# Embedding gather with position add: indices turned on VectorE instead of TensorE, GpSimd as leader, second position load issued earlier

## The chip, the cores and the metric

One core of one Trainium2 chip. The metric is device time in microseconds (us), the median of repeated executions. All executions told here are undisturbed (clock 1.00).

## The reference

```python
batch, seq_len, vocab_size, d_model = 32, 512, 50000, 512
token_embed = embedding_table[indices]          # float32 rows of 2 KB
return (token_embed + position_embed).astype(np.float32)
```

16,384 rows are gathered (33.6 MB), a position row is added to each, and 33.6 MB are stored. The position table is 1 MB, the indices 128 KB as 64-bit words.

## The kernel before

Position p*4+k of a sequence lies on partition p. A *slot* holds one sequence (128 partitions x 4 x 512 float32); there are 23 slots. GpSimd issues one indirect DMA of 128 rows (256 KB) per pair (sequence b, quarter k), 128 in all, with at most 10 in flight. VectorE adds the position row, ScalarE issues the stores.

```python
# ScalarE: loads
nc.scalar.dma_start(out=idx0[:, 0, :], in_=idx_first[:, 0, :]).then_inc(s_first, 16)
load_pos(0)                                    # 512 KB: quarters 0 and 1
nc.scalar.dma_start(out=idx0[:, 1:, :], in_=idx_first[:, 1:, :]).then_inc(s_next, 16)
nc.scalar.dma_start(out=idx_raw[:], in_=...).then_inc(s_raw, 16)   # all indices, 128 KB
nc.scalar.wait_ge(s_pos[0], 16)
load_pos(1)                                    # 512 KB: quarters 2 and 3
# GpSimd
nc.gpsimd.affine_select(out=ident[:], ...)     # identity, for the matmuls
nc.gpsimd.wait_ge(s_first, 16)
for g, (b, k) in enumerate(order):
    if g == half: nc.gpsimd.wait_ge(s_next, 16)
    if g == FIRST * K: nc.gpsimd.wait_ge(s_prep, 2 + K + J)        # indices turned
    ...
    ins = nc.gpsimd.indirect_dma_start(out=slots[b % SLOTS][:, k, :], in_=table, ...)
    ins = ins.then_inc(s_gather[g % LANES], 16)                    # LANES = 10
    if g >= LANES: ins._wait_ge(s_gather[g % LANES], rounds(g - LANES))
# TensorE: four transposes of the indices as float32
# VectorE
for g, (b, k) in enumerate(order):
    if g == 7: tensor_copy(idx_f <- idx_raw)                       # int32 to float32
    if g == 9: four tensor_copy(idx_t <- turned)                   # PSUM float32 to int32
    if b == 0: tensor_copy(pos_ps[:, k, :] <- pos_sb[:, k, :])     # positions into PSUM
    slot += pos_ps[:, k, :]                                        # waits for gather g
# ScalarE: one store for each half sequence (512 KB) as its adds are done
# (cut: the last sequence, and the first halves of sequences 0 and 1, go in quarters)
```

The first four sequences take their indices straight from a small load (idx0). The other 28 need them turned: they are loaded with contiguous rows, and must come to lie with one position per partition.

Of the kernel before, what the change touches and what calls it, by code (L numbers as in the profile page):

```python
# [7 lines left out]
P = 128  # L8
K = 4
# [3 lines left out]
Q = 32  # L13


@with_exitstack
def kernel(
    ctx: ExitStack,
    tc: tile.TileContext,
    indices: bass.AP,  # L20
    embedding_table: bass.AP,
    position_embed: bass.AP,
    out: bass.AP,
):






    nc = tc.nc
    f32 = mybir.dt.float32
    i32 = mybir.dt.int32
    add = mybir.AluOpType.add

    B, S = indices.shape
    V, D = embedding_table.shape
    assert S == P * K and B == 32
    assert V < (1 << 24), "an index passes through float32"
    J = P // Q  # L40


    idx_words = indices.bitcast(i32)
    idx_first = idx_words[0:FIRST].rearrange("b (p w) -> p b w", p=P)
    idx_rows = idx_words.rearrange("b (j w) -> (b j) w", j=J)
    out_rows = out.rearrange("b (p k) d -> b p k d", k=K)
    pos_rows = position_embed.rearrange("(p k) d -> p k d", k=K)
    table = embedding_table[:, :]

    def sbuf(name, shape, dtype):  # L50
        return ctx.enter_context(tc.tile_pool(name="p_" + name, bufs=1)).tile(
            shape, dtype, name=name
        )

    def psum(name, shape, dtype):
        pool = tc.tile_pool(name="p_" + name, bufs=1, space=bass.MemoryType.PSUM)
        return ctx.enter_context(pool).tile(shape, dtype, name=name)

    idx0 = sbuf("idx0", [P, FIRST, 2 * K], i32)
    idx_raw = sbuf("idx_raw", [P, Q * K, 2], i32)  # L60
    ident = sbuf("ident", [P, P], f32)
    idx_f = sbuf("idx_f", [P, Q, K], f32)
    idx_t = sbuf("idx_t", [P, K, B], i32)
    pos_sb = sbuf("pos_sb", [P, K, D], f32)
    slots = [sbuf(f"slot{n}", [P, K, D], f32) for n in range(SLOTS)]
    turned = psum("turned", [Q, K, B, J], f32)
    pos_ps = psum("pos_ps", [P, K, D], f32)



    half = K // 2
    order = [(b, k) for h in range(2) for b in range(FIRST)
             for k in range(h * half, (h + 1) * half)]
    order += [(b, k) for b in range(FIRST, B) for k in range(K)]
    stores = []
    for g, (b, k) in enumerate(order):
        if (b <= 1 and k < half) or b == B - 1:
            stores.append((g + 1, b, k, 1))
        elif k % half == half - 1:
            stores.append((g + 1, b, k + 1 - half, half))  # L80

    sem = tc.alloc_semaphore
    s_first, s_next, s_raw = sem("s_first"), sem("s_next"), sem("s_raw")
    s_pos = [sem(f"s_pos{h}") for h in range(2)]
    s_gather = [sem(f"s_gather{n}") for n in range(LANES)]

    reused = range(B - SLOTS)
    s_out, s_rest = sem("s_out"), sem("s_rest")

    s_prep, s_ps, s_add = sem("s_prep"), sem("s_ps"), sem("s_add")  # L90

    def rounds(g):
        return 16 * (g // LANES + 1)

    def load_pos(h):
        part = slice(h * half, (h + 1) * half)
        nc.scalar.dma_start(out=pos_sb[:, part, :], in_=pos_rows[:, part, :]).then_inc(
            s_pos[h], 16
        )

    with tc.tile_critical(sync_engine=nc.vector.engine, no_gpsimd_drain=True):  # L101


        nc.scalar.dma_start(out=idx0[:, 0, :], in_=idx_first[:, 0, :]).then_inc(
            s_first, 16
        )
        load_pos(0)
        nc.scalar.dma_start(out=idx0[:, 1:, :], in_=idx_first[:, 1:, :]).then_inc(
            s_next, 16
        )  # L110
        nc.scalar.dma_start(
            out=idx_raw[:], in_=idx_rows.rearrange("r (s w) -> r s w", w=2)
        ).then_inc(s_raw, 16)
        nc.scalar.wait_ge(s_pos[0], 16)
        load_pos(1)


        nc.gpsimd.affine_select(  # L118
            out=ident[:], in_=nc.const_aps.tensor(1.0, [P, P], f32),
            pattern=[[-1, P]], compare_op=mybir.AluOpType.is_equal, fill=0.0,  # L120
            base=0, channel_multiplier=1,
        ).then_inc(s_prep, 1)
        nc.gpsimd.wait_ge(s_first, 16)
        for g, (b, k) in enumerate(order):
            if g == half:
                nc.gpsimd.wait_ge(s_next, 16)
            if g == FIRST * K:
                nc.gpsimd.wait_ge(s_prep, 2 + K + J)
            if b == SLOTS and k == 0:
                done = sum(1 for x in stores if x[1] in reused)  # L130
                nc.gpsimd.wait_ge(s_out, 16 * done)
            if b < FIRST:
                where = idx0[:, b, 2 * k : 2 * k + 1]
            else:
                where = idx_t[:, k, b : b + 1]
            ins = nc.gpsimd.indirect_dma_start(  # L136
                out=slots[b % SLOTS][:, k, :],
                out_offset=None,
                in_=table,
                in_offset=bass.IndirectOffsetOnAxis(ap=where, axis=0),  # L140
            ).then_inc(s_gather[g % LANES], 16)
            if g >= LANES:
                ins._wait_ge(s_gather[g % LANES], rounds(g - LANES))
        nc.gpsimd.drain()


        nc.tensor.wait_ge(s_prep, 2)
        for k in range(K):
            nc.tensor.transpose(  # L149
                turned[:, k].rearrange("p b j -> p (b j)"), idx_f[:, :, k], ident[:]  # L150
            ).then_inc(s_prep, 1)


        for g, (b, k) in enumerate(order):
            if g == 7:
                nc.vector.tensor_copy(  # L156
                    out=idx_f[:].rearrange("r p k -> r (p k)"), in_=idx_raw[:, :, 0]
                )._wait_ge(s_raw, 16).then_inc(s_prep, 1)
            if g == 9:
                nc.vector.wait_ge(s_prep, 2 + K)  # L160
                for j in range(J):
                    nc.vector.tensor_copy(  # L162
                        out=idx_t[j * Q : (j + 1) * Q, :, :], in_=turned[:, :, :, j]
                    ).then_inc(s_prep, 1)
            if b == 0:
                nc.vector.tensor_copy(out=pos_ps[:, k, :], in_=pos_sb[:, k, :])._wait_ge(  # L166
                    s_pos[k // half], 16
                ).then_inc(s_ps, 1)
                nc.vector.wait_ge(s_ps, k + 1)
            part = slots[b % SLOTS][:, k, :]  # L170
            nc.vector.tensor_tensor(  # L171
                out=part, in0=part, in1=pos_ps[:, k, :], op=add
            )._wait_ge(s_gather[g % LANES], rounds(g)).then_inc(s_add, 1)


        rest = 0
        for adds, b, at, n in stores:
            done = s_out if b in reused else s_rest
            rest += b not in reused
            nc.scalar.dma_start(  # L180
                out=out_rows[b][:, at : at + n, :],
                in_=slots[b % SLOTS][:, at : at + n, :],
            )._wait_ge(s_add, adds).then_inc(done, 16)
    tc.no_sync_barrier()
    nc.scalar.wait_ge(s_rest, nc.scalar.to_reg(16 * rest))
# [30 lines left out]
```

## Time and profile before

| | value |
|---|---|
| time, median of 6 | 182.02 us (181.74 to 182.42) |
| profiled span | 178.1 us |
| GpSimd busy | 121.8 us (68%) |
| VectorE busy | 91.4 us (51%) |
| moved | 68.34 MB, mean 384 GB/s over the span |

The row of the page that says most is the rate in 40 slices of 4.45 us each:

```profile
GB/s 122 234 329 359 375 378 364 385 410 413 416 416 419 419 419 420 419 420 419 419 420 420 419 419 418 419 418 419 420 419 420 418 420 420 420 419 421 417 258 0
```

The rate takes nine slices (40 us) to pass 400 and thirteen to reach 419, and then stays near there until the last two slices.

### The profile page before, as it was taken

The numbers are of one execution on the slowest core, as the hardware profiler recorded it, in microseconds if no ns is written. First come the engines' busy times: TensorE is split into PE (matmuls) and PEld (weight loads), VectorE is DVE, ScalarE is ACT, GpSimd is POOL, SyncE is SP. The second block draws the span as 40 slices with busy tenths as digits, with TensorE's granted clock in tenths as the row PEclk, the third lists the DMA queues.
The fourth block names the chain that finished last, engine by engine and source line by source line (L and its number), as shares of the span: only waits on it lengthen the run. The fifth ranks groups of instructions, "written<-read, shape, count | busy, mean of one in ns | idle before, by whom it ended". The sixth has DMA issues, their size and how long they took to land.

```text
span 178.1 us, 415 instructions
## 1 busy us (share of the span) xinstructions
PE 1.0 (1%) x4; PEld 0.4 (0%) x4; DVE 91.4 (51%) x137; POOL 121.8 (68%) x133
## 2 busy tenths in 40 slices
PE   0000100000000000000000000000000000000000
PEld 0000000000000000000000000000000000000000
DVE  0445973455556555555556455555556555554510
POOL 3777777777777777777777777777777777774000
DMA  4899999999999999999999999999999999999960
GB/s 122 234 329 359 375 378 364 385 410 413 416 416 419 419 419 420 419 420 419 419 420 420 419 419 418 419 418 419 420 419 420 418 420 420 420 419 421 417 258 0
DMA packets 21011, 68.34 MB, mean 384 GB/s; under 512 B 3728, under 2 KB 3856, under 8 KB 21008
## 3 DMA queue, kind: packets, MB, share of 16 engines
q10 hardware_dynamic: 10768, 34.76, 48.6%
q0 software_dynamic: 10240, 33.56, 48.1%
q14 instruction: 3, 0.02, 0.0%
HBM read 34.75 MB, written 33.55 MB: 384 GB/s over the span
## 4 chain that ended last, share of the span: by engine, by line
POOL 65%; issue 23%; DMA 5%; DVE 2%; ACTq 0%; DVEq 0%
POOL slot L136 65%; DMA slot<-in_embedding_table_dram,idx_t 4%; DVE slot L171 2%; DMA idx<-in_indices_dram 1%; ACTq L211 0%; DVEq L101 0%
## 5 line engine op out<-in xcount | busy, mean ns | idle before, releaser
L136 POOL DMA_INDIRECT slot<-in_embedding_table_dram,idx_t x112 | 106.0, 946 | 34.1 <-issue 34.1
L171 DVE TENSOR_TENSOR slot<-slot,pos_ps 128x512 f32<-128x512 f32 x128 | 87.7, 687 | 73.8 <-issue 57.8
L136 POOL DMA_INDIRECT slot<-in_embedding_table_dram,idx x16 | 15.3, 958 | 6.0 <-issue 4.6
L166 DVE COPY pos_ps<-pos_sb 128x512 f32<-128x512 f32 x4 | 2.7, 685 | 4.9 <-DMA pos_sb<-in_position_embed_dram 4.9
L162 DVE CAST idx_t<-turned 32x128 int32<-32x128 f32 x4 | 1.1, 280 | 0.1
L149 PE MATMUL turned<-ident,idx_f 128*32 128x128 f32 x4 | 1.0, 413 | 17.6 <-issue 17.6
L118 POOL TENSOR_SCALAR_AFFINE_SELECT ident<-const-float32-1.0 128x128 f32<-128x128 f32 x1 | 0.3, 282 | 0.7 <-DVEq L101 0.7
L149 PEld LDWEIGHTS turned<-ident,idx_f 128*32 128x32 f32 x4 | 0.4, 131 | 17.7 <-issue 17.6
L200 POOL MEMSET const-float32-0.0<- 128x1 f32 x1 | 0.1, 99 | 0.3 <-issue 0.3
L156 DVE CAST idx_f<-idx_raw 128x128 f32<-128x128 int32 x1 | 0.2, 220 | 0.0
L200 POOL MEMSET const-uint8-127<- 128x1 uint8 x1 | 0.1, 116 | 0.0
L200 POOL MEMSET const-bfloat16-1.0<- 128x1 bf16 x1 | 0.1, 110 | 0.0
L200 POOL MEMSET const-float32-1.0<- 128x1 f32 x1 | 0.1, 102 | 0.0
## 6 DMA issues: line engine op xcount, KB each, us to landing
out_dram<-slot ACTq DMA_DIRECT2D x60, 512.0 KB
out_dram<-slot ACTq DMA_DIRECT2D x8, 256.0 KB
slot<-in_embedding_table_dram,idx_t POOLq DMA_INDIRECT x112
pos_sb<-in_position_embed_dram ACTq DMA_DIRECT2D x2, 512.0 KB, 4.7
slot<-in_embedding_table_dram,idx POOLq DMA_INDIRECT x16
idx_raw<-in_indices_dram ACTq DMA_DIRECT2D x1, 128.0 KB
idx<-in_indices_dram ACTq DMA_DIRECT2D x1, 4.0 KB, 1.6
idx<-in_indices_dram ACTq DMA_DIRECT2D x1, 12.0 KB
```

Source lines behind the costliest of these rows:

```text
L118: nc.gpsimd.affine_select(out=ident[:], in_=nc.const_aps.tensor(1.0, [P, P], f32), pattern=[[-1, P]], compare_op=mybir.AluOpType.is_equal, ...
L136: ins = nc.gpsimd.indirect_dma_start(out=slots[b % SLOTS][:, k, :], out_offset=None, in_=table, in_offset=bass.IndirectOffsetOnAxis(ap=whe ...
L149: nc.tensor.transpose(turned[:, k].rearrange("p b j -> p (b j)"), idx_f[:, :, k], ident[:]).then_inc(s_prep, 1)
L156: nc.vector.tensor_copy(out=idx_f[:].rearrange("r p k -> r (p k)"), in_=idx_raw[:, :, 0])._wait_ge(s_raw, 16).then_inc(s_prep, 1)
L162: nc.vector.tensor_copy(out=idx_t[j * Q : (j + 1) * Q, :, :], in_=turned[:, :, :, j]).then_inc(s_prep, 1)
L166: nc.vector.tensor_copy(out=pos_ps[:, k, :], in_=pos_sb[:, k, :])._wait_ge(s_pos[k // half], 16).then_inc(s_ps, 1)
L171: nc.vector.tensor_tensor(out=part, in0=part, in1=pos_ps[:, k, :], op=add)._wait_ge(s_gather[g % LANES], rounds(g)).then_inc(s_add, 1)
L200: nc = _bacc.Bacc("TRN2", target_bir_lowering=False, num_devices=1)
```

## The change

Its intent: take the turning of the indices off three engines. If 32 partitions hold 32 sequences, VectorE's transpose of 32 x 32 blocks does the whole turning in one instruction, in int32; identity, cast to float32, four matmuls and four casts back go. The index load becomes four loads for that. GpSimd releases the other engines at the start in place of VectorE, and the second half of the position table is issued right behind the index loads instead of after the first half has landed.

```diff
-    with tc.tile_critical(sync_engine=nc.vector.engine, no_gpsimd_drain=True):
+    with tc.tile_critical(sync_engine=nc.gpsimd.engine, no_gpsimd_drain=True):
...
-        nc.scalar.dma_start(
-            out=idx_raw[:], in_=idx_rows.rearrange("r (s w) -> r s w", w=2)
-        ).then_inc(s_raw, 16)
-        nc.scalar.wait_ge(s_pos[0], 16)
+        for j in range(J):
+            nc.scalar.dma_start(
+                out=idx_raw[j * B : (j + 1) * B, :], in_=idx_rows[:, j, :]
+            ).then_inc(s_raw, 16)
         load_pos(1)
-        nc.gpsimd.affine_select(out=ident[:], ...)
...
-                nc.gpsimd.wait_ge(s_prep, 2 + K + J)
+                nc.gpsimd.wait_ge(s_idx, 1)
...
-        (four nc.tensor.transpose, one cast to float32, four casts back)
+                nc.vector.transpose(
+                    out=idx_t[:],
+                    in_=idx_raw[:].rearrange("r (q k w) -> r k q w", k=K, w=2)[:, :, :, 0],
+                )._wait_ge(s_raw, 16 * J).then_inc(s_idx, 1)
```

More of the change, by code (lines that the diff above doesn't have):

```diff
@@ L38 @@
     assert S == P * K and B == 32
-    assert V < (1 << 24), "an index passes through float32"
     J = P // Q
+    assert B == Q, "indices are turned in squares of 32"
     idx_words = indices.bitcast(i32)
     idx_first = idx_words[0:FIRST].rearrange("b (p w) -> p b w", p=P)
-    idx_rows = idx_words.rearrange("b (j w) -> (b j) w", j=J)
+    idx_rows = idx_words.rearrange("b (j w) -> b j w", j=J)
     out_rows = out.rearrange("b (p k) d -> b p k d", k=K)
@@ L59 @@
     idx0 = sbuf("idx0", [P, FIRST, 2 * K], i32)
-    idx_raw = sbuf("idx_raw", [P, Q * K, 2], i32)
-    ident = sbuf("ident", [P, P], f32)
-    idx_f = sbuf("idx_f", [P, Q, K], f32)
+    idx_raw = sbuf("idx_raw", [P, 2 * Q * K], i32)
     idx_t = sbuf("idx_t", [P, K, B], i32)
@@ L65 @@
     slots = [sbuf(f"slot{n}", [P, K, D], f32) for n in range(SLOTS)]
-    turned = psum("turned", [Q, K, B, J], f32)
     pos_ps = psum("pos_ps", [P, K, D], f32)
@@ L88 @@
     s_out, s_rest = sem("s_out"), sem("s_rest")
-    s_prep, s_ps, s_add = sem("s_prep"), sem("s_ps"), sem("s_add")
+    s_idx, s_ps, s_add = sem("s_idx"), sem("s_ps"), sem("s_add")
     def rounds(g):
@@ L110 @@
         )
-        nc.scalar.dma_start(
-            out=idx_raw[:], in_=idx_rows.rearrange("r (s w) -> r s w", w=2)
-        ).then_inc(s_raw, 16)
-        nc.scalar.wait_ge(s_pos[0], 16)
+        for j in range(J):
+            nc.scalar.dma_start(
+                out=idx_raw[j * B : (j + 1) * B, :], in_=idx_rows[:, j, :]
+            ).then_inc(s_raw, 16)
         load_pos(1)
-        nc.gpsimd.affine_select(
-            out=ident[:], in_=nc.const_aps.tensor(1.0, [P, P], f32),
-            pattern=[[-1, P]], compare_op=mybir.AluOpType.is_equal, fill=0.0,
-            base=0, channel_multiplier=1,
-        ).then_inc(s_prep, 1)
         nc.gpsimd.wait_ge(s_first, 16)
@@ L144 @@
         nc.gpsimd.drain()
-        nc.tensor.wait_ge(s_prep, 2)
-        for k in range(K):
-            nc.tensor.transpose(
-                turned[:, k].rearrange("p b j -> p (b j)"), idx_f[:, :, k], ident[:]
-            ).then_inc(s_prep, 1)
         for g, (b, k) in enumerate(order):
             if g == 7:
-                nc.vector.tensor_copy(
-                    out=idx_f[:].rearrange("r p k -> r (p k)"), in_=idx_raw[:, :, 0]
-                )._wait_ge(s_raw, 16).then_inc(s_prep, 1)
-            if g == 9:
-                nc.vector.wait_ge(s_prep, 2 + K)
-                for j in range(J):
-                    nc.vector.tensor_copy(
-                        out=idx_t[j * Q : (j + 1) * Q, :, :], in_=turned[:, :, :, j]
-                    ).then_inc(s_prep, 1)
+                nc.vector.transpose(
+                    out=idx_t[:],
+                    in_=idx_raw[:].rearrange("r (q k w) -> r k q w", k=K, w=2)[
+                        :, :, :, 0
+                    ],
+                )._wait_ge(s_raw, 16 * J).then_inc(s_idx, 1)
             if b == 0:
```

## The prediction

> **What bounds the kernel now**
>
> I read the page first: the engine rows, the sliced DMA row and the groups of instructions.
>
> ```profile
> PE 1.0 (1%) x4; PEld 0.4 (0%) x4; DVE 91.4 (51%) x137; POOL 121.8 (68%) x133
> ...
> DMA  4899999999999999999999999999999999999960
> ...
> L136 POOL DMA_INDIRECT slot<-in_embedding_table_dram,idx_t x112 | 106.0, 946 | 34.1 <-issue 34.1
> ...
> L162 DVE CAST idx_t<-turned 32x128 int32<-32x128 f32 x4 | 1.1, 280 | 0.1
> ```
>
> No compute engine is full, the DMA engines are. GpSimd spends 0.946 us on a gather and then a constant 0.30 us (34.1 / 112) of "issue": one gather of 256 KB every 1.25 us, with no wait between. That is 262,144 B / 1.252 us = 209 GB/s of gather, and as much again of stores, 419 GB/s. So two limits lie on each other. To see which of them sets the end I cut the span into stretches (columns: length, busy time of PE, PEld, DVE, POOL, clock, DMA share, GB/s).
>
> ```profile
> 2.50:10.50 8.00, 0.00 (x0) 0.00 (x0) 2.25 (x4) 5.87 (x6) 1.00 0.86 240
> 10.50:20.00 9.50, 1.04 (x4) 0.43 (x4) 5.98 (x11) 7.28 (x8) 1.00 1.00 380
> 20.00:30.00 10.00, 0.00 (x0) 0.00 (x0) 6.56 (x13) 7.56 (x9) 1.00 0.99 360
> 30.00:40.00 10.00, 0.00 (x0) 0.00 (x0) 4.82 (x8) 7.57 (x9) 1.00 1.02 400
> 50.00:160.00 110.00, 0.00 (x0) 0.00 (x0) 60.39 (x89) 83.19 (x89) 1.00 1.03 419
> 164.00:168.00 4.00, 0.00 (x0) 0.00 (x0) 2.54 (x4) 0.00 (x0) 1.00 1.03 420
> 171.00:173.50 2.50, 0.00 (x0) 0.00 (x0) 0.00 (x0) 0.00 (x0) 1.00 0.44 170
> ```
>
> The row 164 to 168 decides it: GpSimd has issued its last gather (162.9), and the DMA engines still run at 420 GB/s on what is queued. In the timeline the last gather is issued at 161.94, but the last add starts at 169.59, 7.65 us later; the first gather needed 3.78 us (issued 2.89, added 6.67). About 4 us of transfers were therefore queued when GpSimd finished. Since supply in the middle (419) equals capacity (420), this queue, built in the first 40 us, is never worked off. Bytes lost early are paid at the end: 68.34 MB at 420 GB/s are 162.7 us; data flows from 2.5 to about 173, so some 8 us are lost. Per stretch, length x (420 - rate) / 420: 3.4 us in 2.5 to 10.5, 0.9 in 10.5 to 20, 1.4 in 20 to 30, 0.5 in 30 to 40, 1.5 after 171.
>
> Then the timeline, first around the start, then around 20 us, for what the change touches (start, duration).
>
> ```profile
> 1.03 0.38 ACTq L104 DMA_DIRECT2D idx<-in_indices_dram  x1
> 1.44 0.45 ACTq L97 DMA_DIRECT2D pos_sb<-in_position_embed_dram  x1
> 1.93 0.46 ACTq L108 DMA_DIRECT2D idx<-in_indices_dram  x1
> 2.41 0.51 ACTq L111 DMA_DIRECT2D idx_raw<-in_indices_dram  x1
> 2.89 1.14 POOL L136 DMA_INDIRECT slot<-in_embedding_table_dram,idx  x1 [1.43 <-DMA idx<-in_indices_dram]
> ...
> 4.93 0.33 ACTq L97 DMA_DIRECT2D pos_sb<-in_position_embed_dram  x1
> ...
> 10.23 0.69 DVE L171 TENSOR_TENSOR slot<-slot,pos_ps 128x512 f32<-128x512 f32 x1 [2.27 <-DMA slot<-in_embedding_table_dram,idx]
> ...
> 19.86 1.21 DVE L162 CAST idx_t<-turned 32x128 int32<-32x128 f32 x4
> ...
> 23.30 0.69 DVE L171 TENSOR_TENSOR slot<-slot,pos_ps 128x512 f32<-128x512 f32 x1 [0.25 <-issue]
> ```
>
> The first gather waits for the first index load; the second half of the positions is issued at 4.93, when the first has landed; the second add comes 3.6 us after the first because gather 1 shares the engines with it; and from 17.83 to 23.05 VectorE has no gap of note, so here it delays stores. The gathers that use the turned indices start at 23.09 with the usual 0.30 us before them: the turning is not on GpSimd's path.
>
> **What the Trainium skill says**
>
> "DMA: Bandwidth & Descriptors", section "Queues, rings and completion order": each DMA engine takes turns between the queues that have work, a packet at a time. That agrees with 6 to 8 us, where the DMA view shows both queues at work (52% of engine time the position load's queue, 21% the gathers'). The same page, "Rules for kernel authors", says of transfers split over partition ranges "Don't bother — they serialize"; no trace here shows it yet, the 128 KB index load being one DMA so far. "VectorE: DVE Perf Modes", section "The three transpose paths": VectorE turns 32 x 32 blocks only, 311 ns for 128 x 128 of bf16. Blocks are all that is needed once each group of 32 partitions holds the 32 sequences; this case has no duration for it yet. "Runtime: NRT & Kernel Launch", section "Instruction fetch mechanics": a sequencer fetches its instructions by DMA, mostly hidden. The DMA view has one instruction packet between 169.5 and 170.5, and in that time the last store is issued at 171.10, 0.82 us after its add ended (170.28), where the store before it followed its add (169.33) by 0.03.
>
> **The change part by part**
>
> 1. *GpSimd leads.* Now VectorE releases the others, and GpSimd is seen to wait 0.7 us for it. GpSimd is also the engine that finishes the constants (0.52 us), so one hop falls away. A hop is about 0.05 to 0.1 us (VectorE's row releases ScalarE, whose first load is at 1.03). I take 0.1 us: first load at 0.93, first gather at 2.79, all else follows. On the path: -0.1.
>
> 2. *Identity, cast, four matmuls, four casts go; one transpose comes.* The identity (0.28) and the matmuls (1.0) lie on idle engines: 0. VectorE loses 0.22 + 1.21 = 1.43 us and gains one transpose of 128 elements per partition; the cast of the same 128 x 128 took 0.22 and the page's figure is 0.31, so 0.3 as an estimate: net -1.1 us, in the stretch 17.3 to 23 where VectorE is behind. Adds 8 to 10 and their stores come up to 1.1 us earlier. DMA was not empty then, only slow (360 instead of 420 GB/s), so I credit about a third: -0.4 of the 1.4 us lost in 20 to 30.
>
> 3. *Index load in four.* Three more issues on ScalarE, each 0.4 to 0.5 (steps between the rows 1.03, 1.44, 1.93, 2.41): the fourth part is issued near 3.7, the same 128 KB. VectorE wants it only at 17. Path: 0.
>
> 4. *Second position half behind the index loads.* Start 2.41 - 0.1 + 4 x 0.46 = about 4.15 instead of 4.93: 0.8 us earlier. It then meets gather 0 still in flight: first add later by up to 0.5 us (512 KB + 256 KB at some 330 GB/s instead of 256 KB alone), but it is gone about 1 us earlier, so gathers 1 to 3 and their stores come forward by 0.5 to 1 us. Of the 3.4 us lost before 10.5 I credit -0.4.
>
> 5. *Tail.* ScalarE's stream grows by three loads and loses a wait. If the 0.8 us before the last store is its instruction fetch, the fetch moves to an earlier store with queued work behind it. Expected: 40% x 0.8 = -0.3.
>
> Sum: -0.1 - 0.4 - 0.4 - 0.3 = -1.2 us; 181.99 - 1.2 = 180.8.
>
> **The rivals**
>
> A: nothing but the hop is gained, because DMA bytes are unchanged and the engines are busy from 8 us on; the earlier position load only delays gather 0, and the earlier stores take turns from gathers. Speaks for it: DMA share of 0.99 to 1.03 from 10.5 us. Against: those busy engines moved 360 GB/s, not 420. Result 181.9.
>
> B: all credits come in full: 1.1 us of VectorE, 0.8 of the position load, 0.8 of the tail and 0.1, that is 2.8 us, 179.2. It is near a floor: GpSimd's 128 x 1.25 = 160.2 us are untouched, its last issue still ends near 162.8, and last gather to last add cannot be under the 3.8 us of the first; the last add would then start at 165.7 instead of 169.6, 3.9 us sooner. "Faster by over 2%" needs 3.64 us, so nearly all of the queue would have to vanish.
>
> C: it gets slower: the position half delays the first gathers and the first store by 0.5 us without return, and a fetch lands worse: 182.6.
>
> **Range and chances**
>
> Most weight lies between A and B: 180.8, range 179.8 to 182.0. Repeats of the kernel before spread by 0.7 us, which is in the range. Faster by over 2% (under 178.35) 0.03, slower by over 2% (over 185.63) 0.01, within 2% 0.96.
>
> **What would show it**
>
> Right: the same 1.25 us gather rhythm; first gather near 2.8; second position load near 4.2; second add before 9.7; VectorE with a gap before 21; 250 to 270 GB/s in 2.5 to 10.5 and 370 or more in 20 to 30; last add 0.8 to 1.2 us earlier than 169.59. Step 5 shows in the gap between last add and last store: under 0.1 us if the fetch was it. Wrong: a first gather later than 2.9, a gather waiting for turned indices at 23, a transpose over 1 us, or a gather rhythm that changes; a shorter rhythm alone, 128 times, could bring over 2%.

## The result, and the profile after

| | before | after |
|---|---|---|
| time, median of 6 | 182.02 us | 182.35 us (182.08 to 182.46) |
| profiled span | 178.1 us | 178.8 us |

The ratio is 1.0014 (95% interval 1.0000 to 1.0027). A ratio is the mean time of one kernel's runs over that of the other's in the same rounds, so it is not quite the ratio of the medians. The change gained nothing; 1.2 us had been predicted, with 182.0 as the upper edge.

The page of the changed kernel, first the engine row, then the gathers and the new instruction:

```profile
DVE 90.5 (51%) x133; POOL 121.4 (68%) x132
...
L126 POOL DMA_INDIRECT slot<-in_embedding_table_dram,idx_t x112 | 105.9, 946 | 34.1 <-issue 34.1
...
L139 DVE STREAM_TRANSPOSE idx_t<-idx_raw 128x128 int32<-128x128 int32 x1 | 0.4, 401 | 0.0
```

The mean gather rhythm is the same to the nanosecond (946 ns and 34.1 us of pauses), TensorE is gone from the page, VectorE lost 0.9 us.

The same stretches of the changed kernel (columns: length, busy time of VectorE and GpSimd with counts, clock, DMA share, GB/s):

```profile
2.50:10.50 8.00, 2.55 (x4) 5.79 (x6) 1.00 0.93 282
10.50:20.00 9.50, 5.51 (x10) 7.27 (x8) 1.00 0.98 347
20.00:30.00 10.00, 5.54 (x9) 7.56 (x9) 1.00 1.00 355
30.00:40.00 10.00, 5.41 (x8) 7.56 (x9) 1.00 1.02 406
50.00:160.00 110.00, 59.84 (x87) 83.19 (x89) 1.00 1.03 418
```

The rate before 10.5 us rose from 240 to 282 GB/s, 336 KB more in 8 us, which is 0.8 us of transfer at 420. In the next stretch it fell from 380 to 347 GB/s, 314 KB less. What was gained before 10.5 us was gone at 20.

The timeline of the changed kernel, start and end (start, duration, engine, line, what, idle before):

```profile
2.28 1.92 ACTq L107 DMA_DIRECT2D idx_raw<-in_indices_dram  x4
2.81 1.08 POOL L126 DMA_INDIRECT slot<-in_embedding_table_dram,idx  x1 [2.36 <-DMA idx<-in_indices_dram]
...
4.23 0.45 ACTq L93 DMA_DIRECT2D pos_sb<-in_position_embed_dram  x1
...
5.61 0.94 POOL L126 DMA_INDIRECT slot<-in_embedding_table_dram,idx  x1 [0.47 <-issue]
...
8.08 0.69 DVE L151 TENSOR_TENSOR slot<-slot,pos_ps 128x512 f32<-128x512 f32 x1 [2.18 <-DMA slot<-in_embedding_table_dram,idx]
...
9.93 1.92 DVE L151 TENSOR_TENSOR slot<-slot,pos_ps 128x512 f32<-128x512 f32 x3 [0.56 <-DMA slot<-in_embedding_table_dram,idx]
...
161.90 0.95 POOL L126 DMA_INDIRECT slot<-in_embedding_table_dram,idx_t  x1 [0.30 <-issue]
...
170.14 0.69 DVE L151 TENSOR_TENSOR slot<-slot,pos_ps 128x512 f32<-128x512 f32 x1 [0.45 <-issue]
```

And the end of the kernel before:

```profile
161.94 0.94 POOL L136 DMA_INDIRECT slot<-in_embedding_table_dram,idx_t  x1 [0.30 <-issue]
...
169.59 0.69 DVE L171 TENSOR_TENSOR slot<-slot,pos_ps 128x512 f32<-128x512 f32 x1 [0.27 <-issue]
```

GpSimd starts 0.08 us earlier, loses it again at gather 2 (0.47 us of pause instead of 0.30; by the program it waits there for the next index load, though the trace names no releaser), and issues the last gather only 0.04 us earlier. The first add comes 1.4 us later (8.08 instead of 6.67), the second 0.3 us earlier (9.93 instead of 10.23). The last add is 0.55 us later.

A useful measure from such a timeline is the **lag**: from the start of a gather on GpSimd to the start of its add on VectorE. Its mean over gathers 60 to 107 was 7.88 us before and 7.45 us after. So in mid-run the changed kernel was ahead by 0.4 us. From about gather 112 on its lag grew to 8.2 to 8.4 us. In these two executions, then, an early lead existed and did not last. Executions of one kernel differ by as much, as the runs below show, so this pair alone does not make it a gain of the kernel.

### The profile page after: what moved, and what is told of

It reads as the page before. It is cut to its first block, busy times and chain, and to the rows that moved or that the text cites. A ratio compares the mean times of both kernels' runs of the same rounds, so it can differ in the third digit from the quotient of the medians.

```text
span 178.8 us, 399 instructions
## 1 busy us (share of the span) xinstructions
DVE 90.5 (51%) x133; POOL 121.4 (68%) x132
## 4 chain that ended last, share of the span: by engine, by line
POOL 65%; issue 23%; DMA 6%; DVE 1%; POOLq 1%; ACTq 0%
POOL slot L126 65%; DMA slot<-in_embedding_table_dram,idx_t 5%; DVE slot L151 1%; DMA idx<-in_indices_dram 1%; POOLq L134 1%; ACTq L191 0%; POOLq L97 0%; POOLq L180 0%
## 5 line engine op out<-in xcount | busy, mean ns | idle before, releaser
L126 POOL DMA_INDIRECT slot<-in_embedding_table_dram,idx_t x112 | 105.9, 946 | 34.1 <-issue 34.1
```

## The experiments

Every test kernel needed one more edit than is told: the last wait for the stores compares with a register, in a form that could not be used for new kernels here, so it was put inside the critical section with a constant. The first two runs are the controls for that. All runs had 5 rounds; a line "lag" is the mean over gathers 60 to 107, worked out from the timeline as above. Kernels are compared only within the same rounds.

The theories. **B** is the prediction's: the DMA engines are the bound, each byte not moved early is paid at the end at 420 GB/s. **D** was formed after the first four runs, whose expectations speak of a narrower "theory 1" (the early position half gives back what it gains) in its place: the engines reach 419 GB/s only while enough gathers and stores are queued; an early gain just means that they run short for longer until that much is queued, and the end follows GpSimd's chain of gathers.

### Controls

```diff
-    nc.scalar.wait_ge(s_rest, nc.scalar.to_reg(16 * rest))   # after the critical section
+        nc.scalar.wait_ge(s_rest, 16 * rest)                 # its last instruction
```

> Control: the kernel before, with the last wait on the stores put inside the critical section as a constant, which all test kernels need. All theories: ratio to before 0.998 to 1.003; the first add near 6.7, mid-run time from a gather's issue to its add near 7.8 us as in the kernel before. If the ratio is outside, it is the new reference for the others.

> Control: the changed kernel with the same constant wait. All theories: ratio to the control of before 1.000 to 1.003 (the changed kernel itself had 1.0014). If the loss of some 0.9 us that its profile shows after 140 us (gather to add grows from 7.4 to 8.2 us) belongs to the kernel, it is in this profile too, at the same place; if it is chance of one execution, it is not.

Measured, on a chip where the kernel before takes 176.48 us: control of before 176.25 us, ratio 0.9987 (0.9962 to 1.0011), lag 8.0 us; control of after 176.67 us, ratio 0.9996 (0.9969 to 1.0024), lag 7.95 us; the last gather is issued at 161.92 and 161.81. The two controls cannot be told apart. The late loss of the changed kernel's first profile is not seen again at that place: here the lag is about 8 from the middle on and 8.2 over the last eight gathers, so most of that loss looks like chance of that execution. In the control of before ScalarE issues the last store 0.03 us after the last add, as in the changed kernel, so comparisons with this control leave the tail (step 5) out. Executions of one kernel spread by about 1.2 us here, so 0.3% is the least that these runs resolve.

### The second position half alone, and all but it

```diff
 # pos_only, on the kernel before
-        nc.scalar.wait_ge(s_pos[0], 16)
         load_pos(1)
 # undo_pos, on the changed kernel
+        nc.scalar.wait_ge(s_pos[0], 16)
         load_pos(1)
```

> Kernel before with one edit: no wait ahead of the second position half, so it is issued at about 2.9 instead of 4.93. Theory 1 (the early half takes turns from gather 0, and what it gains before 10 us is given back because stores start later): first add near 8, first store after 8, rate above 260 GB/s in 2.5 to 10.5 but below 365 in 10.5 to 20, time within 0.5 us of the control, so nothing gained. Rival (the early half is good by itself and another part of the change took the gain back): 0.5 to 1 us faster than the control of before.

> Changed kernel with the wait ahead of the second position half put back (one part undone). Theory 1: first add back near 6.7, 2.5 to 10.5 back near 240 GB/s, time within 0.5 us of the control of before. Rival (the early half is what gains, the rest costs): slower than the changed control by 0.5 us or more. Second rival (the earlier lead, the turning on VectorE and the shifted instruction fetch are worth their 0.8 us and the early half eats them): 0.5 to 0.8 us faster than both controls.

Measured: pos_only 176.65 us, ratio 1.0026 (1.0003 to 1.0050); undo_pos 176.66 us, ratio 1.0018 (0.9987 to 1.0048). In pos_only the first add starts at 8.37, 2.5 to 10.5 us runs at 285 GB/s and 10.5 to 20 at only 312: what theory 1 expected, and nothing gained. In undo_pos the time is as expected too, but not the trace: with the wait back, the second half is issued at 4.87, yet the first add still starts at 8.03 and 2.5 to 10.5 us runs at 276 GB/s. So the early half is not the only thing that delays the first add (one execution each). What does in undo_pos is open: turn_only below has the same four index loads and its first add at 6.75. For the time it does not matter.

### Less to move at the start, less in the middle, more in the middle

```diff
 # no_pos1: second half never loaded, first half added instead (wrong result on purpose)
-        nc.scalar.wait_ge(s_pos[0], 16)
-        load_pos(1)
-   ... in_=pos_sb[:, k, :])._wait_ge(s_pos[k // half], 16)
+   ... in_=pos_sb[:, k % half, :])._wait_ge(s_pos[0], 16)
 # skip_mid: two stores of 512 KB left out near 90 us (wrong result on purpose)
         for adds, b, at, n in stores:
+            if b == 16:
+                continue
 # extra_mid: ahead of each of the same two stores, one more load of 512 KB
+            if b == 16:
+                nc.scalar.dma_start(out=pos_sb[:, part, :], in_=pos_rows[:, part, :])
+                    ._wait_ge(s_add, adds).then_inc(s_more, 16)
```

> Kernel before (constant wait) without the second position load at all; the first half is added in its place, so the result is wrong on purpose. 512 KB less for the DMA engines in the first 10 us. Theory B (the prediction's: every byte not moved early is paid at the end, at 420 GB/s): 524 KB / 420 GB/s = 1.25 us faster, ratio 0.993. Theory D (the engines run short until enough gathers and stores are queued; an early gain is used up again before 50 us, and the end follows GpSimd's chain): 0 to 0.4 us faster, ratio 0.998 to 1.0, with the time from a gather's issue to its add back at 7.3 to 8 us after 50 us.

> Kernel before (constant wait) without the two stores of sequence 16, so 1.05 MB less to move near 90 us; wrong result on purpose. Theory B: 2.5 us faster, ratio 0.986, and the time from gather to add drops by about 2.5 us near 90 us and stays there to the end. Theory D: it drops and climbs back to 7 us or more within some 20 to 30 us, and the time is 0 to 0.8 us faster, ratio 0.9955 to 1.0.

> Kernel before (constant wait) with 1.05 MB more to move near 90 us: the position table is loaded once more, to the same place with the same values. Both theories: supply (419) leaves no room to work off more than the queue needs, so gather to add rises by about 2.5 us near 90 us and stays; 2.0 to 2.5 us slower, ratio 1.011 to 1.014. If it falls back instead, the engines had room to spare and the queue is of another making: ratio 1.0 to 1.003.

Measured, on another chip of the faster kind (kernel before 176.27 us): no_pos1 176.34 us, ratio 1.0009 (0.9982 to 1.0035); skip_mid 176.12 us, ratio 0.9991 (0.9964 to 1.0019); extra_mid 179.04 us, ratio 1.0153 (1.0126 to 1.0181). Theory B asked 0.993 and 0.986 of the first two: it falls. The stretches of no_pos1 (columns as in the prediction) show the gain being used up. First the control of before in 10.5 to 20, then no_pos1:

```profile
10.50:20.00 9.50, 1.04 (x4) 0.43 (x4) 6.42 (x11) 7.24 (x8) 1.00 1.00 363
```

```profile
2.50:10.50 8.00, 0.00 (x0) 0.00 (x0) 3.36 (x5) 5.87 (x6) 1.00 0.83 249
10.50:20.00 9.50, 1.04 (x4) 0.43 (x4) 5.01 (x9) 7.27 (x8) 1.00 0.94 315
20.00:30.00 10.00, 0.00 (x0) 0.00 (x0) 6.43 (x13) 7.56 (x9) 1.00 1.00 371
...
80.00:90.00 10.00, 0.00 (x0) 0.00 (x0) 5.49 (x8) 7.57 (x9) 1.00 1.03 419
```

With half a megabyte less to do, the engines moved 315 GB/s in 10.5 to 20, less than the 363 of the control. By 50 us the lag was 7.3 us, where it stayed. In skip_mid the same is to be seen in the middle of the run, with nothing else going on:

```profile
60.00:90.00 30.00, 0.00 (x0) 0.00 (x0) 16.38 (x24) 22.69 (x25) 1.00 1.03 418
90.00:100.00 10.00, 0.00 (x0) 0.00 (x0) 6.81 (x12) 7.56 (x9) 1.00 1.01 392
100.00:110.00 10.00, 0.00 (x0) 0.00 (x0) 3.60 (x6) 7.56 (x9) 1.00 1.00 369
110.00:120.00 10.00, 0.00 (x0) 0.00 (x0) 5.84 (x9) 7.56 (x9) 1.00 1.02 413
120.00:160.00 40.00, 0.00 (x0) 0.00 (x0) 21.98 (x32) 30.25 (x33) 1.00 1.03 417
```

GpSimd's column does not change (9 gathers in 10 us). The rate drops to 369 GB/s after the stores are left out, with a DMA share of 1.00: a share near 1 does not mean a full rate. The lag falls from 7.4 (gather 69) to 4.3 (gather 74) and is back at 7.8 four gathers later; it dips once more to 6.5 and ends at 7.4.

How can busy engines move less? The queue lines of the DMA view (packets, MB, share of 16 engines) answer it in part; here the gathers' queue of skip_mid in 80 to 90 and in 100 to 110 us, then of lanes_5 (below) in 50 to 150:

```profile
q0 software_dynamic: 637, 2.09, 51.3%
q0 software_dynamic: 519, 1.70, 51.6%
q0 software_dynamic: 5684, 18.63, 53.7%
```

Share x 16 engines x time / packets gives 129 ns for a gather packet at 419 GB/s, 159 ns at 369 and 151 ns at 373, at the same mean size of 3.3 KB; the stores' packets stay at 142 to 144 ns. So in the slow stretches the engines are occupied and each gather packet takes longer. Why it does is not shown.

Added work behaves otherwise: in extra_mid the lag climbs by 2.5 us and stays (10.7 at the end), and 2.8 us are paid (2.2 to 3.2), about the 1.05 MB / 419 GB/s = 2.5 us that it takes to move. The supply is 419 GB/s, the rate on a full queue 420 (164 to 168 us of the kernel before), and nothing of the added work was worked off.

### GpSimd's chain later

```diff
         nc.gpsimd.wait_ge(s_first, 16)
+        nc.gpsimd.wait_ge(s_pos[0], 16)
```

> Kernel before (constant wait) with GpSimd's first gather held until the first position half has landed, so its whole chain starts and ends about 2.1 us later; the same bytes. Theory D: the end follows the chain one for one, 1.8 to 2.2 us slower, ratio 1.010 to 1.0125. Theory B: the position halves move undisturbed meanwhile, so less is lost in 2.5 to 20 us and only part is paid, 0.8 to 1.6 us slower, ratio 1.0045 to 1.009.

Measured, same chip: 179.27 us, ratio 1.0170 (1.0143 to 1.0197), 3.0 us slower. The delay came out larger than planned, and the first gather started at 5.99. The ends of the control and of late_start:

```profile
161.92 0.95 POOL L136 DMA_INDIRECT slot<-in_embedding_table_dram,idx_t  x1 [0.30 <-issue]
...
170.00 0.69 DVE L171 TENSOR_TENSOR slot<-slot,pos_ps 128x512 f32<-128x512 f32 x1 [0.44 <-DMA slot<-in_embedding_table_dram,idx_t]
```

```profile
164.98 0.95 POOL L137 DMA_INDIRECT slot<-in_embedding_table_dram,idx_t  x1 [0.30 <-issue]
...
172.49 0.69 DVE L172 TENSOR_TENSOR slot<-slot,pos_ps 128x512 f32<-128x512 f32 x1 [0.43 <-DMA slot<-in_embedding_table_dram,idx_t]
```

The chain ends 3.06 us later and the median time is 3.0 us longer (2.5 to 3.5 by the interval): one for one, as theory D says. Theory B's 0.8 to 1.6 for 2.1 us of delay would be 1.2 to 2.4 for 3.06. The last add of these two profiles is only 2.49 us later, because the control's profile is of its longest execution (176.91 us, lag 8.0; late_start 7.4).

### The single parts on VectorE and GpSimd, and less at the very end

```diff
 # skip_late: as skip_mid, with sequence 30 (wrong result on purpose)
+            if b == 30:
+                continue
 # dve_lag: three more copies of 128x512 into unused PSUM, ahead of the casts
             if g == 9:
+                for n in range(3):
+                    nc.vector.tensor_copy(out=spare[n][:], in_=pos_sb[:, 0, :])
 # turn_only: the changed kernel with VectorE as leader and the wait ahead of load_pos(1)
 # lead_only: the kernel before with sync_engine=nc.gpsimd.engine
```

> Kernel before (constant wait) without the two stores of sequence 30, so 1.05 MB less to move at the very end; wrong result on purpose. Theory D (an early or middle gain is used up within some 12 us, so only one inside the last 12 us is left): 1.5 to 2.5 us faster, ratio 0.986 to 0.9915, where the same bytes taken out near 90 us gave nothing. Rival (the end is a fixed chain, DMA bytes never matter): 0 to 0.4 us faster.

> Kernel before (constant wait) with three more copies of 128x512 on VectorE near 20 us (about 2.1 us) into unused PSUM: the opposite of what the change takes off VectorE there (1.0 us net). Prediction's step 2 (a third of what VectorE loses there is paid): 0.6 to 0.8 us slower, ratio 1.0035 to 1.0045. Theory D: adds near 20 to 25 us late by up to 2 us, the time within 0.3 us of the control, ratio 0.998 to 1.002.

> Only the turning changed: four index loads and VectorE's transpose, no identity, casts or matmuls; VectorE leads and the second position half waits as before. Prediction's step 2: 0.3 to 0.5 us faster. Theory D: within 0.3 us of the control, ratio 0.998 to 1.002; last gather issued at 161.9 to 162.1.

> Only the leader changed, to GpSimd. Theory D: the end follows the chain, which starts about 0.1 us earlier and keeps it only if the second gather finds the next index load landed; 0 to 0.15 us faster, below what these runs resolve, ratio 0.998 to 1.002. Rival (GpSimd as leader costs something at the exit): 0.3 us or more slower, with a later exit after the last store has landed.

These four ran on a chip of the slower kind (kernel before 182.15 us): skip_late 182.33 us, ratio 1.0017 (0.9996 to 1.0038); dve_lag 182.68 us, ratio 1.0029 (1.0013 to 1.0044); turn_only 182.58 us, ratio 1.0022 (1.0007 to 1.0037); lead_only 182.34 us, ratio 1.0016 (0.9999 to 1.0032). By their times, none gains. But the times of this chip can hardly be read at this size. On the faster chips, the time of an execution is its span plus 1.7 to 1.8 us in every run (176.91 and 175.2; 175.93 and 174.2). Here spans of 177.2 to 182.4 us stand beside times of 181.94 to 182.93. The trace shows what lies behind the last store: at the end SyncE takes about 0.7 us for each of its last instructions, where on the faster chips it takes 0.02. In skip_late ScalarE's wait for the last store was over at 172.11, 1.3 us before that in the first profile of the kernel before (173.41), and the time did not follow. All four kernels also lacked a control with the constant wait on this chip, so their 0.2% is not evidence against a part either. dve_lag failed as a test for another reason: its copies stood ahead of the casts, the turned indices came late, and GpSimd's last gather moved to 163.53 (ScalarE's wait was over at 174.60, later too).

### The three that were open

```diff
 # skip_late2: the same kernel as skip_late, on a faster chip
 # dve_lag2: the three copies behind the casts (at g == 10), so that the indices are not late
 # lanes_5
-LANES = 10
+LANES = 5
```

> The same kernel as skip_late (sequence 30 not stored, wrong on purpose), hoped for on a chip where the time follows the kernel's end. Theory D: 1.0 to 2.5 us faster, ratio 0.986 to 0.9945, ScalarE's release after the last store at or before 172.2. Rival (fixed chain): 0 to 0.4 us faster, release at 173 or later.

> As dve_lag, but the three extra copies stand behind the casts, so the turned indices are not late and GpSimd's chain is untouched (last gather issued at 161.9 to 162.1). Prediction's step 2: 0.6 us or more slower, ratio over 1.0035. Theory D: adds 10 to 14 late by up to 2 us, the time within 0.4 us, ratio 0.998 to 1.0023.

> Kernel before (constant wait) with 5 gathers in flight at most instead of 10, so a gather's issue to its add cannot exceed some 6.3 us. Theory D in its strong form (the engines need more than 6 us of work queued to run at 419 GB/s): GpSimd waits for gathers, below 415 GB/s in 50 to 150 us, 2 us or more slower. Rival (the queue is a leftover, fewer in flight do as well): GpSimd waits only until the leftover is gone, 419 GB/s after, time within 0.5 us or up to 1 us faster since less is queued at the end.

Measured, on the chip of no_pos1 (kernel before 176.27 us):

skip_late2: 175.22 us, ratio 0.9943 (0.9915 to 0.9971), 1.0 us faster, ScalarE's release at 172.45. The same 1.05 MB that gave nothing near 90 us are worth 1.0 us at the end. That is at the lower edge of what D now expected, 0.25 us later than the release named, and clear of the rival. For skip_late D had asked 1.5 to 2.5 us; that first range is missed.

dve_lag2: 176.74 us, ratio 1.0027 (1.0003 to 1.0051), so about 0.5 us lost (0.05 to 0.9), between the two expectations and not settled by the time alone. The timeline shows VectorE's three copies, then six adds in a row to catch up:

```profile
22.80 1.87 DVE L168 COPY spare<-pos_sb 128x512 f32<-128x512 f32 x3
24.58 3.66 DVE L175 TENSOR_TENSOR slot<-slot,pos_ps 128x512 f32<-128x512 f32 x6
29.67 0.69 DVE L175 TENSOR_TENSOR slot<-slot,pos_ps 128x512 f32<-128x512 f32 x1 [1.42 <-DMA slot<-in_embedding_table_dram,idx_t]
```

The last gather is issued at 161.97 as ever, but the lag is 8.5 to 8.8 us from about 53 us to the end, 0.7 more than in the control. But the profile is of the slowest of the six executions (177.35). A delay may stick where a gain does not; extra_mid shows it plainly, this run only suggests it.

lanes_5: 191.82 us, ratio 1.0913 (1.0854 to 1.0971), 15.5 us slower. Its gathers and one stretch, the columns as before:

```profile
L136 POOL DMA_INDIRECT slot<-in_embedding_table_dram,idx_t x112 | 105.9, 946 | 50.4 <-DMA slot<-in_embedding_table_dram,idx_t 32.9 <-issue 16.6 <-DMA slot<-in_embedding_table_dram,idx 1.0
```

```profile
50.00:150.00 100.00, 0.00 (x0) 0.00 (x0) 48.63 (x72) 68.19 (x73) 1.00 1.00 373
```

With at most 5 gathers in flight (mean lag 6.6 us) the engines move 373 GB/s instead of 417 to 419, with a share of 1.00, and GpSimd waits 33 us for gathers. So 5 are too few for the full rate, and the queue is not all leftover. How many are needed was not tried: 6 to 9, and more than 10, stay open.

No run points to a version that beats both kernels: no part of the change shortens GpSimd's chain, and the lag of 7.3 us that the better executions show is the least mean that any run shows together with 419 GB/s. Nor was a shorter gather rhythm tried.

## Why the prediction was wrong, point by point

**The frame.** Right: two limits lie on each other, 1.25 us per gather and 420 GB/s, and what is queued above need is never worked off (extra_mid paid in full). Wrong, and this is the step that failed: "Bytes lost early are paid at the end". It was read from the profile as a sum, and the sum does hold for each profile. But it was used as if the lost bytes could be won back one by one. no_pos1 and skip_mid took 0.5 and 1.05 MB out and won nothing where 1.25 and 2.5 us were due. The low rates of 10.5 to 40 us last until the lag is about 7 us, and the gains made early in these runs prolonged them. The time is GpSimd's last issue (161.8 to 162.2 in every kernel whose chain was left alone), plus a lag of 7.3 to 8.7 us, plus the last store.

How much of the queue could have been won at all? The prediction took 7.65 - 3.78 = 4 us of it for winnable. On the faster chips, in the seven profiles with the chain untouched and the tail complete (before_c, after_c, pos_only, undo_pos, no_pos1, skip_mid, dve_lag2), the time of the profiled execution less its mean lag over gathers 108 to 127 is 168.5 to 168.9 us, while the times run from 175.83 to 177.35 and the lags from 7.27 to 8.70: an execution is as long as the lag it settles in. The kernel before, at 176.3 to 176.5 us, thus has a typical lag of 7.4 to 8.0 us (an estimate from these figures), and only 0.1 to 0.7 us of it lie above the least lag of these profiles. The 0.8 us credited to steps 2 and 4 would have needed a lag under 7.3, and no run held one at the full rate: when skip_mid forced it to 4.3, the rate fell to 369 GB/s until it was back. Whether 7.3 is a floor was not tested further.

**Step 1, leader.** Right in kind: ScalarE's first load moved from 1.03 to 0.90, the first gather from 2.89 to 2.81. The leader is not alone in this: turn_only, with VectorE leading, has its first load at 0.96 and first gather at 2.82, lead_only 0.96 and 2.95, and without either the first gather starts anywhere from 2.89 to 3.15. Of the 0.1 us, 0.04 was left at the last gather, because gather 2 then had to wait for the next index load.

**Step 2, turning.** The transpose took 0.40 us (0.3 estimated), VectorE lost 0.9 us (1.1 estimated), VectorE caught up at 22.2 us instead of 23.05, not before 21 as named (its one earlier gap, 0.73 us before the add at 18.12, waits for a gather). The credit of 0.4 us was wrong: 20 to 30 us went from 360 to 355 GB/s. Being late there may cost (dve_lag2); that being early gains nothing rests on after_c and undo_pos, which have other parts too, since turn_only ran on the slower chip.

**Step 3, index load in four.** Four issues took 1.92 us of ScalarE instead of 0.51, and cost no time that a run could resolve.

**Step 4, second position half.** Issued at 4.23, as reckoned (4.15). The rate before 10.5 us rose even more than named (282; 250 to 270 expected). But the first add came 1.4 us later where "up to 0.5" stood. The prediction's own figures do not give 0.5: 512 KB at 330 GB/s are 1.6 us if they go first, 0.8 if both loads share evenly. In the changed kernel 0.24 of gather 0's 0.26 MB had moved by 6.0 us; from 6.0 to 7.0 the gathers' queue moved 0.01 MB and the other, the position load, 0.32, so the rest of gather 0 came late. The second add came at 9.93 where "before 9.7" stood, and 10.5 to 20 us lost what had been won. The credit of 0.4 us was 0 within what pos_only resolves (it came out 0.05 to 0.9 us slower).

**Step 5, tail.** Right in fact: the pause between the last add and the last store went from 0.82 to 0.03 us, and the instruction packet moved from 169.96 to 164.73. Worth little at most: the last store was issued at 170.86 instead of 171.10, into engines that still had stores to move, and ScalarE's wait was over at 173.77 instead of 173.41. From the end of the last add to there passed 2.94 us instead of 3.13; runs without the pause show 2.71 to 3.28, so the 0.2 us between them is not evidence of a gain.

**The rivals.** By its reason A was nearest ("nothing but the hop is gained", 181.9): earlier work takes turns from other work. By its number C was (182.6 against 182.35), but by luck as far as is known: the late first add it named came, the worse instruction fetch did not, and the 0.3 us slower is not explained. B (179.2) is out. The argument held against A, that busy engines at 360 GB/s must have room, was the mistake: skip_mid shows 369 GB/s at a share of 1.00 with less to do.

**The 0.3 us by which it is slower.** Open. It was measured on a chip of the slower kind, whose times hardly follow the kernel's own end, and on a faster chip the two controls do not differ. That chip would also have hidden much of a true gain.

## What to carry to other kernels

A low rate while a pipeline fills is not a stock of lost time: ask whether the engines had work queued, and test it by taking work out, because here a gain in front of a fixed-rate producer was used up again within some ten transfers. Look for the chain that paces the producer (here 128 gathers of 1.25 us on GpSimd): delaying its start cost its full 3 us, and less to move paid only at the very end (1.0 us of 2.5). Shortening that chain was not tried, and here it would meet the DMA rate of 420 GB/s. Compare the forecast gain with how far executions of one kernel differ in the same quantity. When a DMA-bound kernel limits its transfers in flight, vary that number early: 5 instead of 10 cost 15.5 us.

## What the Trainium skill lacked or had wrong

- "DMA: Bandwidth & Descriptors", which gives rates by transfer size, has no figure for how many gathers must be in flight: with 5 gathers of 256 KB allowed beside the stores the rate was 373 GB/s, with 10 allowed 417 to 419, at a DMA share of 1.00 and 1.03. Nor has it a packet's time by load: a gather packet took 151 ns and 130 ns there.
- "VectorE: DVE Perf Modes", section "The three transpose paths", gives 311 ns for 128 x 128 of bf16 and none for 32-bit data: the int32 transpose of 128 x 128 from a strided input took 401 ns.
- No page has it: the same kernel takes 176.3 to 176.5 us on two chips and 182.0 to 182.2 us in the other two measurements, with the same gather rhythm (946 ns); in the slower ones SyncE's last instructions take about 0.7 us each instead of 0.02, and times hardly follow the end of the kernel's own work.
